# A ninth Strassen step in four projection units, and joins by transfer in the output units

## The chip, the cores and the metric

The kernel runs on one NeuronCore of a Trainium2 chip. TensorE (PE) multiplies: a stationary operand of 128x128 is loaded into its array (the trace shows these loads as PEld) and up to 512 columns stream past it into a bank of PSUM. VectorE (DVE) and ScalarE (ACT) work elementwise on SBUF and PSUM. SyncE (SP) issues the loads of the weights, GpSimd (POOL) issues most other transfers and runs a few small operations. Every engine takes its own instructions in order; they wait for each other by semaphores.

The metric is the device time of the program in microseconds (us), as the median of several runs.

## The reference

A decoder block for 256 tokens of width 4096, all in float32:

```python
h = rmsnorm(x, norm_w)
proj = h @ w_in                                    # 256 x 4096 times 4096 x 20480
u_p, z_p, u_c, b_c, c_c, z_c, g_logit = split(proj)    # six of 2048, one of 8192
y_pool = causal_multiscale_pool(u_p, pool_w, pool_scale) * silu(z_p)
y_conv = causal_gated_shortconv(u_c, b_c, c_c, conv_w, conv_b) * silu(z_c)
br = [y_pool @ w_branch[0], y_conv @ w_branch[1]]  # 256 x 2048 times 2048 x 4096, twice
merged = sum(sigmoid(g_logit + gate_b) * br)
out = rmsnorm(x + merged @ w_out, final_norm_w)    # 256 x 4096 times 4096 x 4096
```

The pooling averages over 2, 4, 8 or 16 trailing tokens by channel group, subtracts the token itself and applies a 512x512 matrix to each group. The short convolution has three taps.

## The kernel before

**Units and steps.** Every product is cut into units of 1024 output columns. Twenty units belong to `w_in` (`cz`, `cb`, `cu`, `cc` for the convolution, twice; `pz`, `pu` for the pooling, twice; `g0_0` to `g1_3` for the gates), eight to `w_branch` (`b0_0` to `b1_3`) and four to `w_out` (`o0` to `o3`). They run in that order. A unit of `w_in` or `w_out` has 16 steps, one for each pair of 128-row blocks of the inner dimension; a step loads one weight tile of 128 x 2048 (1 MB), which holds four quarters of 512 columns.

**Precision.** Each operand is split into a rounded high part and a low part, and each product takes three matmuls (high by high, high by low, low by high). For a weight tile ACT writes the high parts (`highs`, line 222, through `act`, line 60) and DVE the low parts (`lows`, line 226, through `sub`, which records at line 63).

**P and S steps.** A plain step (P) multiplies four quarters for two token halves: 8 groups of 3 matmuls. A Strassen step (S) forms four sums of the weight quarters and needs 7 groups of 3: M2, N3, M1, N7, N5, N6, N4, in this order unless it is the unit's last step. S uses the four operand entries of the pair of blocks themselves and four sums of them (Q3, Q5, Q6, Q7). For eight of the sixteen pairs of `x` (or of the merged tensor) the sums lie ready in `arena`; for the pairs 6 and 7 they can be put into a small tile `side`. The texts at the top name the order of steps: `EIGHT` has eight S of sixteen, `NINE`, `NINE_A` and `NINE_B` nine, `TEN` ten, `OUT3` seven, always with three P at its end.

**The ring.** High and low parts of weight quarters and of their sums go into a ring of `CELLS = 15` cells. A P step takes 4 cells, an S step 3 and then 4. Cells are given out in circular order and a request waits until all its cells are free (`Ring`, line 196). A cell is freed by the group that reads it last. `pump` (line 983) lays out the preparation of later steps as far ahead as cells allow, in program order, between the groups of matmuls. A P step right behind an S step is rounded in two halves.

**Joins.** The S products that belong to several quarters gather in four banks (`shared`); at a unit's end ACT copies them to a join slot, DVE forms three sums there (`corner_sums`), and `combine` (line 420) adds the slot to the unit's result. A unit marked `late` does this by two accumulating transfers from POOL, the others by an operation on DVE. A unit that `rotates` takes one of the three weight buffers (`raw`) as its slot; others use a tile of their own. `o0`, `o1` and `o2` rotate and are not late.

**Epilogues.** What follows a unit's end is a queue of small items, one taken at every sixth matmul (a tick), so that it runs beside the next unit. `gap(n)` are n empty ticks. In `g0_0`'s epilogue, which runs beside `g1_0`, the side sums of pair 6 and then of pair 7 are formed: a load of the pair into `sa` at once, scaling by ACT 8 ticks later, sums by DVE, and a store. In `pz0` and `pz1` the epilogue, beside `pu0` and `pu1`, builds the pooling bands; its last item are six small operations of DVE (line 75 and 629 in the trace).

**pu.** `pu0` and `pu1` have the text `EIGHT`. Side sums stand in `side` from `cz0` on, but the tile's place is given to the bands before `pu0`; the pooling itself (steps B and M) is multiplied inside `pz1` and `g0_0`.

**Fills.** The operands of the branch units and of the output units are refilled from memory through staging buffers (`sa`, and from `g1_3` on also `sb`): a transfer, four sums on DVE where the pair is an S pair, a rounding on ACT and a subtraction on DVE (`Fill`, line 768; `pop_fill`, line 799). `stages` (line 794) lists the buffers.

Of the kernel before, what the change touches and what calls it, by code (L numbers as in the profile page):

```python
# [44 lines left out]
TEN = "PSPSSPSSPSSPSSPS"  # L45
OUT3 = "PSPSPSPSPSPSSPPP"
B0 = "PPPPSPSP"
# [5 lines left out]
def hybrid_block(ctx: ExitStack, tc: tile.TileContext, x, xc, prm, rows_in, w_in, pool_w, w_branch, w_out, out):  # L53
# [185 lines left out]
    class Step:  # L239
        def __init__(self, unit, kind, src=None, op=None, **kw):  # L240
            self.unit, self.kind, self.src, self.op = unit, kind, src, op
            self.__dict__.update(kw)
            self.raw = None
            self.prepared = self.halved = False
            self.pre, self.mid = [], []

# [71 lines left out]
        def groups(self):  # L318
# [20 lines left out]
            else:  # L339
# [10 lines left out]
                for nm in order:  # L350
                    o, cell, bank = prods[nm]
                    ah, al = self.op.entry(o)
                    mm = [(ah, high(cell)), (ah, low(cell)), (al, high(cell))]
                    gs.append([bank, mm, [cell]])
            return gs

# [144 lines left out]

    def seq_x(text):
        if text is FIRST:
            return [("P", i) for i in FIRST]
        ns = text.count("S")
        if ns > NS + NB:
            ps, ss = list(range(16 - ns)), list(range(ND, 16)) + [ND - 1]
            if text is TEN:
                tens.append(text)
                ss = [ND - 2 + len(tens) % 2] + ss[:-1] + [ND - 1 - len(tens) % 2]  # L510
            return [(c, (ss if c == "S" else ps).pop(0)) for c in text]
        return sequence(text, ND, ND + NS + NB, NB)
# [3 lines left out]

    def in_unit(name, col, epi, text, **kw):
        units.append(Unit(name, lambda i: w_in[col // NU, i], seq_x(text), x_ops, epi, scaled=True, **kw))
        units[-1].text = text
        return units[-1]  # L520

    def side_items(i=ND - 1):
        def scaled():
            for k in range(2):
                v = sa[:, 6 - 2 * k:8 - 2 * k]
                act(v, v, scale=norm_col(2 * i + k))

        return [lambda: move(sa[:, 4:].rearrange("p o c -> p (o c)"), xc[i])] + gap(7) + [scaled, None, lambda: sums_s(sa)] + gap(3) + [
            lambda: act(side["tile"][:, 0], sa[:, 0:4]), None,
            lambda: sub(side["tile"][:, 1], sa[:, 0:4], side["tile"][:, 0].bitcast(F32))]  # L530

# [9 lines left out]
    def conv_units(c, first):  # L541
# [7 lines left out]
        def c_epi(u):  # L549
# [22 lines left out]
        u = in_unit(f"cz{c}", base + 3 * HALF, lambda u: silu_y(u.late) + (gap(4) + side_items() if first else []),  # L572
                    FIRST if first else SIX4, dst=Y)
# [106 lines left out]
    def gate_unit(n, c):  # L680
        def epi(u):
# [52 lines left out]
    def out_unit(c):  # L734
# [17 lines left out]

# [40 lines left out]

    stages = [sa]
    fills = deque()
# [3 lines left out]
    def pop_fill(force=None):  # L799
# [7 lines left out]
        if nxt is None or not nxt.ready() or now[0] < hush[0]:  # L807
            return
        st = next((q for q in stages if not any(q is u for u in used)), None)
        if st is not None:  # L810
# [115 lines left out]
    def before(i, fn, *args):  # L926
        steps[i].pre.append(item(fn, *args))

    for j in range(16):
# [163 lines left out]
    for u in units:  # L1093
# [3 lines left out]
        if not u.rotates:  # L1097
            u.join.slot = quarters(Y if u.name[0] == "g" else spare() if u.name[0] == "b" else E)
        if u is names["g1_0"]:
            bands_open.close()  # L1100
            open_side()
        if u is last_x:
            side["stack"].close()
            more = ctx.enter_context(tc.tile_pool(name="more", bufs=1))
            stages.append(more.tile([P, 8, P], F32, name="sb"))
            queue_fills()
        if u is last:
            break
        for st in u.steps:
            assert st.prepared, (u.name, st.kind)  # L1110
            run_step(u, st)
            if u.text is TEN and st.kind == "S" and st.op in x_ops[:ND] and st is not u.steps[-1]:
                move(side["tile"], side_d[ND - 1 - x_ops.index(st.op)])
            state["now"] += 1
# [114 lines left out]
```

## Time and profile before

| | |
|---|---|
| median of 3 runs | 2378.08 us (2377.83 to 2378.94) |
| the profiled run's own time | 2378.31 us |
| its span in the profile | 2376.6 us |
| granted TensorE clock, mean | 0.998 |
| PE busy | 2358.6 us (99%), 10466 matmuls |
| DVE busy | 2178.6 us (92%) |
| ACT busy | 1519.3 us (64%) |
| POOL busy | 116.8 us (5%) |
| read from memory, written | 522.51 MB, 27.26 MB |

The page of the profile gives busy time, share and number of instructions by engine, then the span in 40 slices (a digit is the busy share in tenths, PEclk the clock that PE was granted), then the chain of work that ended last. A row of a timeline reads: start in us, duration, engine, line of the program, operation, output and inputs with their shape, how many of them, and in brackets the idle time before with what ended it. The names are those of the program's tiles: `ring`, `raw` (weight buffers), `parts` (the sums of quarters), `arena` (operands), `sums` and `shared` (banks of PSUM). A wait row names who waited for whom, the total, how often, and the longest. Ends of matmuls are modelled, so a row of n matmuls that follow each other is read by the distance between starts.

### The profile page before, as it was taken

The page shows a single profiled execution, that of the slowest core. Times are in us where ns is not written, and L with a number is a line of the kernel's source. Part 1 is how long each engine was busy: PE and PEld are TensorE (multiplying, and loading weights), DVE is VectorE, ACT ScalarE, POOL GpSimd, SP SyncE. Part 2 cuts the span into 40 slices and gives each one's busy share as a digit, 9 for nine tenths or more (in the row PEclk, how much of TensorE's full clock was granted, in tenths as well). Part 3 has the DMA queues.
Part 4 walks back from the last instruction along what each step waited for, and adds up shares of the span by engine and source line. Part 5 has one row for each costly group of instructions (what it writes and reads, how often), then busy time and mean ns, then how long its engine had stood idle before and what let it go on. Part 6 is the DMA issues. An engine that isn't in the chain of part 4 may idle for free.

```text
span 2376.6 us, 28235 instructions
## 1 busy us (share of the span) xinstructions
PE 2358.6 (99%) x10466; PEld 1945.8 (82%) x10466; DVE 2178.6 (92%) x2378; ACT 1519.3 (64%) x1801; POOL 116.8 (5%) x181
## 2 busy tenths in 40 slices
PE   9999999999999999999999999999999999999998
PEld 7888888888888888888788888888888888888886
DVE  8889989989989969969899999998898799899998
ACT  6666656756656656656676767667665566566664
POOL 0000000000001000000000000001100000000000
PEclk9999999999999999999999999999999999999999
DMA  9656646756657546746877787778766666767767
GB/s 344 230 193 235 223 164 260 238 191 236 224 178 269 211 174 221 240 174 217 259 248 251 264 260 250 248 272 274 267 253 242 248 237 239 257 211 252 259 218 267
DMA packets 91322, 564.20 MB, mean 237 GB/s; under 512 B 10096, under 2 KB 10352, under 8 KB 30256
## 3 DMA queue, kind: packets, MB, share of 16 engines
q1 hardware_dynamic: 69824, 485.39, 56.5%
q0 software_dynamic: 20784, 75.77, 11.9%
q8 instruction: 82, 1.34, 0.2%
q10 hardware_dynamic: 576, 1.24, 0.1%
q14 instruction: 56, 0.46, 0.1%
HBM read 522.51 MB, written 27.26 MB: 231 GB/s over the span
## 4 chain that ended last, share of the span: by engine, by line
PE 94%; DVE 3%; DMA 1%; ACT 1%; issue 0%; POOL 0%; SPq 0%; DVEq 0%; ACTq 0%; POOLq 0%
PE sums L1021 69%; PE shared L1021 23%; DVE ring L63 1%; PE shared L665 1%; PE shared L458 1%; DMA sa<-in_xc_dram 1%; DVE parts L63 1%; DMA raw<-in_w_in_dram 1%; ACT ring L60 0%; DVE E L63 0%; DVE raw L63 0%; ACT E L60 0%; DVE E L75 0%; ACT raw L60 0%; PE shared L641 0%
## 5 line engine op out<-in xcount | busy, mean ns | idle before, releaser
L1021 PE MATMUL sums<-ring,arena 128*128 128x512 f32 x7215 | 1687.1, 390 | 4.2 <-DVE ring L63 1.8
L1021 PEld LDWEIGHTS sums<-ring,arena 128*128 128x128 f32 x7215 | 1352.8, 188 | 288.4 <-DVE ring L63 3.1
L63 DVE TENSOR_TENSOR ring<-raw,ring 128x1024 fp32r<-128x1024 f32 (+3 forms) x879 | 971.9, 1126 | 137.2 <-ACT ring L60 136.1
L60 ACT ACTIVATE ring<-raw 128x1024 fp32r<-128x1024 f32 (+3 forms) x682 | 796.2, 1202 | 251.7 <-PE sums L1021 101.2
L60 ACT ACTIVATE ring<-parts 128x512 fp32r<-128x512 f32 (+1 forms) x638 | 476.5, 761 | 475.1 <-DVE parts L63 413.8
L1021 PE MATMUL shared<-ring,arena 128*128 128x512 f32 x2169 | 523.2, 389 | 0.3 <-DVE ring L63 0.3
L63 DVE TENSOR_TENSOR ring<-parts,ring 128x1024 fp32r<-128x1024 f32 (+1 forms) x442 | 492.0, 1158 | 6.1 <-ACT ring L60 6.1
L1021 PEld LDWEIGHTS shared<-ring,arena 128*128 128x128 f32 x2169 | 407.0, 188 | 85.5 <-DVE ring L63 0.8
L63 DVE TENSOR_TENSOR parts<-parts,raw 128x512 f32<-128x512 f32 x416 | 286.6, 689 | 0.0
L63 DVE TENSOR_TENSOR parts<-raw 128x1024 f32<-128x1024 f32 x208 | 254.0, 1221 | 5.5 <-DMA raw<-in_w_in_dram 5.4
L1021 PE MATMUL sums<-ring,last_pair 128*128 128x512 f32 x336 | 84.6, 396 | 0.8 <-DVE ring L63 0.8
L1021 PEld LDWEIGHTS sums<-ring,last_pair 128*128 128x128 f32 x336 | 63.1, 188 | 16.3 <-DVE ring L63 1.2
L1021 PE MATMUL shared<-ring,last_pair 128*128 128x512 f32 x192 | 47.6, 397 | 0.0
L1021 PEld LDWEIGHTS shared<-ring,last_pair 128*128 128x128 f32 x192 | 36.1, 188 | 8.7
L60 ACT ACTIVATE E<-sums 128x512 f32<-128x512 f32 x72 | 39.7, 595 | 5.5 <-PE sums L1021 3.6
L60 ACT ACTIVATE E<-sums,rin 128x512 f32<-128x512 f32 x28 | 17.7, 689 | 29.3 <-PE sums L1021 29.3
L1021 PE MATMUL shared<-ring,side 128*128 128x512 f32 x135 | 34.0, 396 | 0.0
L63 DVE TENSOR_TENSOR raw<-raw 128x512 f32<-128x512 f32 (+1 forms) x27 | 23.5, 870 | 9.8 <-ACT raw L60 8.9
L1021 PEld LDWEIGHTS shared<-ring,side 128*128 128x128 f32 x135 | 25.4, 188 | 6.0
L60 ACT ACTIVATE last_pair<-shared 128x512 f32<-128x512 f32 x44 | 23.9, 596 | 9.4 <-PE shared L458 8.9
L63 DVE TENSOR_TENSOR E<-E,Y 128x2048 f32<-128x2048 f32 x13 | 29.8, 2290 | 0.1
L63 DVE TENSOR_TENSOR E<-E,last_pair 128x2048 f32<-128x2048 f32 x12 | 27.4, 2286 | 2.2 <-ACT E L60 2.2
(134 smaller groups left out, 717.1 us busy)
## 6 DMA issues: line engine op xcount, KB each, us to landing
raw<-in_w_in_dram SPq DMA_DIRECT2D x318, 1024.0 KB, 4.9
raw<-in_w_branch_dram SPq DMA_DIRECT2D x64, 1024.0 KB, 4.9
raw<-in_w_out_dram SPq DMA_DIRECT2D x64, 1024.0 KB, 5.1
E<-in_rows_dram POOLq DMA_DIRECT2D x16, 512.0 KB, 9.8
gates_d<-E POOLq DMA_DIRECT2D x8, 1024.0 KB, 6.1
E<-Y POOLq DMA_DIRECT2D x14, 512.0 KB, 8.2
Y<-E POOLq DMA_DIRECT2D x10, 512.0 KB, 8.1
y_d<-E POOLq DMA_DIRECT2D x8, 512.0 KB, 6.4
```

The lines of the kernel that those rows point to most:

```text
L60: return pin(nc.scalar.activation(dst, src, func, **kw))
L63: return pin(nc.vector.tensor_tensor(out=dst, in0=a, in1=b, op=op))
L458: pin(nc.tensor.transpose(shared(j)[:, i * T + t * P:i * T + (t + 1) * P], src[:, t, c:c + P], ident))
L665: pin(nc.tensor.matmul(o, a, b, start=(k, i) == (0, 0), stop=(k, i) == (3, 2)))
L1021: pin(nc.tensor.matmul(ps, lhs, rhs, start=n == 0, stop=n == u.total[b] - 1))
```

## The change

Five things are changed.

1. `pu0` and `pu1` get the text `NINE_B`. The ninth S step uses pair 7; `at=4` puts it in fifth place among the S steps, which is the ninth step of the unit and stands behind another S step. Its four sums are loaded by POOL from `side_d[1]` into one ring cell (`stream`); the cell is allotted before the step ahead of it and freed with the step's last group. `cz0`'s epilogue now also stores the sums of pair 7 to `side_d[1]`.
2. In `g0_0`'s epilogue only pair 6 is worked; its load stands `HUSH` = 14 ticks later, and pair 7 is loaded ready-made at the end.
3. `o1` and `o2` get `NINE`, with pair 7's sums in a `side` tile that is filled during `o1`; `OUT3` gets an eighth S, so that three S steps follow each other.
4. `o0`, `o1` and `o2` no longer rotate and become late: the slot is `Y`, and two transfers add it to the result. The final weights' row is loaded into `Y` later, and the squares come 8 ticks later.
5. From `g1_3` on half of `Y` serves as a third staging buffer for 40 ticks.

```diff
-OUT3 = "PSPSPSPSPSPSSPPP"
+OUT3 = "PSPSPSPSSPSSSPPP"
...
                 for nm in order:
                     o, cell, bank = prods[nm]
-                    ah, al = self.op.entry(o)
+                    if self.streamed is not None and o < 4:
+                        c = slice(o * P, (o + 1) * P)
+                        ah, al = ring[:, self.streamed, 0, c], ring[:, self.streamed, 1, c]
+                    else:
+                        ah, al = self.op.entry(o)
                     mm = [(ah, high(cell)), (ah, low(cell)), (al, high(cell))]
                     gs.append([bank, mm, [cell]])
+                if self.streamed is not None:
+                    gs[-1][2].append(self.streamed)
...
+            if at:
+                ss.insert(at, ss.pop())
...
             lambda: act(side["tile"][:, 0], sa[:, 0:4]), None,
-            lambda: sub(side["tile"][:, 1], sa[:, 0:4], side["tile"][:, 0].bitcast(F32))]
+            lambda: sub(side["tile"][:, 1], sa[:, 0:4], side["tile"][:, 0].bitcast(F32)),
+            lambda: move(side_d[i - ND + 2], side["tile"])]
...
-        in_unit(f"pu{c}", c * NU, lambda u: [], EIGHT).urgent = lambda: None
+        in_unit(f"pu{c}", c * NU, lambda u: [], NINE_B, at=4).urgent = lambda: None
...
             if (n, c) == (0, 0):
-                sides = []
-                for i in range(ND - 2, ND):
-                    sides += side_items(i) + [lambda i=i: move(side_d[i - ND + 2], side["tile"])]
-                items += gap(len(sides) - len(items))
+                sides = gap(HUSH) + side_items(ND - 2) + [lambda: side_load(ND - 1)]
...
-            return gap(1) + [lambda: row(0), lambda: row(1)] + gap(14) + [
+            return gap(2) + [lambda: row(0), lambda: row(1)] + gap(12) + [start] + gap(8) + [
                 lambda: square(0), lambda: square(1),
                 lambda: mul(E, E, Y[:, 0:1].to_broadcast([P, 2, NU])), lambda: move(o_d[c], E)]
 
-        text = (SIX5, EIGHT, EIGHT, OUT3)[c]
-        units.append(Unit(f"o{c}", lambda i: w_out[c, i], seq_x(text), m_ops, epi, before=start))
+        text = (SIX5, NINE, NINE, OUT3)[c]
+        u = Unit(f"o{c}", lambda i: w_out[c, i], seq_x(text), m_ops, epi, before=start if c == 3 else None)
+        u.late, u.rotates = c < 3, c == 3
+        units.append(u)
...
+    def stream(step, src):
+        def fetch(cells):
+            step.streamed = cells[0]
+            move(ring[:, cells[0]], src.rearrange("p a o c -> p a (o c)"))
+        steps[steps.index(step) - 1].pre.append((1, None, fetch))
+
+    for c in range(2):
+        for st in names[f"pu{c}"].main:
+            if st.kind == "S" and st.op is x_ops[ND - 1]:
+                stream(st, side_d[1])
...
         if not u.rotates:
-            u.join.slot = quarters(Y if u.name[0] == "g" else spare() if u.name[0] == "b" else E)
+            u.join.slot = quarters(Y if u.name[0] in "go" else spare() if u.name[0] == "b" else E)
+        if u is names["o1"]:
+            assert not fills
+            more.close()
+            open_side()
+
+            j, items = ND - 1, list(queue)
+            queue.clear()
+            sides = (gap(HUSH) + [lambda: move(sa[:, 4:].rearrange("p o c -> p (o c)"),
+                                                   m_d[j // 4][:, j % 4].rearrange("p k t -> p (k t)"))] + gap(8) + [
+                lambda: sums_s(sa), None, None, lambda: act(side["tile"][:, 0], sa[:, 0:4]), None,
+                lambda: sub(side["tile"][:, 1], sa[:, 0:4], side["tile"][:, 0].bitcast(F32))])
...
-            stages.append(more.tile([P, 8, P], F32, name="sb"))
+            stages.append((more.enter_context(tc.tile_pool(name="more", bufs=1)).tile([P, 8, P], F32, name="sb"), None))
+            stages.append((Y[:, 0].rearrange("p (o c) -> p o c", c=P), now[0] + 40))
             queue_fills()
```

More of the change, by code (lines that the diff above doesn't have):

```diff
@@ L244, in __init__ @@
             self.prepared = self.halved = False
+            self.streamed = None
             self.pre, self.mid = [], []
@@ L500, in sequence, with seq_x @@
         return [(c, (ss if c == "S" else ps).pop(0)) for c in text]
-    def seq_x(text):
+    def seq_x(text, at=None):
         if text is FIRST:
@@ L515, in seq_y, with in_unit, side_load, side_items @@
         return sequence(text, 8 - text.count("S"), 8, 0)
-    def in_unit(name, col, epi, text, **kw):
-        units.append(Unit(name, lambda i: w_in[col // NU, i], seq_x(text), x_ops, epi, scaled=True, **kw))
+    def in_unit(name, col, epi, text, at=None, **kw):
+        units.append(Unit(name, lambda i: w_in[col // NU, i], seq_x(text, at), x_ops, epi, scaled=True, **kw))
         units[-1].text = text
         return units[-1]
-    def side_items(i=ND - 1):
+    def side_load(i):
+        move(side["tile"], side_d[i - ND + 2])
+    def side_items(i):
         def scaled():
@@ L570, in c_epi @@
             return items + [lambda: move(E, g_d[c])] + gap(6) + [lambda: mul(E, E, Y), lambda: put(y_d[1, c], chan(E))]
-        u = in_unit(f"cz{c}", base + 3 * HALF, lambda u: silu_y(u.late) + (gap(4) + side_items() if first else []),
+        u = in_unit(f"cz{c}", base + 3 * HALF, lambda u: silu_y(u.late) + (gap(4) + side_items(ND - 1) if first else []),
                     FIRST if first else SIX4, dst=Y)
@@ L792, in advance @@
             return True
-    stages = [sa]
+    stages = [(sa, None)]
     fills = deque()
@@ L808, in pop_fill @@
             return
-        st = next((q for q in stages if not any(q is u for u in used)), None)
+        st = next((q for q, t in stages if (t is None or now[0] < t) and not any(q is u for u in used)), None)
         if st is not None:
@@ L1097, in hybrid_block @@
         if not u.rotates:
-            u.join.slot = quarters(Y if u.name[0] == "g" else spare() if u.name[0] == "b" else E)
+            u.join.slot = quarters(Y if u.name[0] in "go" else spare() if u.name[0] == "b" else E)
[9 more added lines that the diff above has]
+                lambda: sub(side["tile"][:, 1], sa[:, 0:4], side["tile"][:, 0].bitcast(F32))])
+            items += gap(len(sides) - len(items))
+            sides += gap(len(items) - len(sides))
+            queue.extend([lambda a=a, b=b: (a and a(), b and b()) for a, b in zip(items, sides)])
         if u is names["g1_0"]:
@@ L1103, in hybrid_block @@
             side["stack"].close()
-            more = ctx.enter_context(tc.tile_pool(name="more", bufs=1))
-            stages.append(more.tile([P, 8, P], F32, name="sb"))
+            more = ExitStack()
+            ctx.enter_context(more)
+            stages.append((more.enter_context(tc.tile_pool(name="more", bufs=1)).tile([P, 8, P], F32, name="sb"), None))
+            stages.append((Y[:, 0].rearrange("p (o c) -> p o c", c=P), now[0] + 40))
             queue_fills()
@@ L1112, in hybrid_block @@
             if u.text is TEN and st.kind == "S" and st.op in x_ops[:ND] and st is not u.steps[-1]:
-                move(side["tile"], side_d[ND - 1 - x_ops.index(st.op)])
+                side_load(2 * ND - 3 - x_ops.index(st.op))
             state["now"] += 1
```

## The prediction

> **What bounds the kernel now.** I read the page's busy times and slices first, then the chain that ended last, then what the matmul engine waited for, and last the timeline around those waits.
>
> ```profile
> span 2376.6 us, 28235 instructions
> PE 2358.6 (99%) x10466; PEld 1945.8 (82%) x10466; DVE 2178.6 (92%) x2378; ACT 1519.3 (64%) x1801; POOL 116.8 (5%) x181
> PE   9999999999999999999999999999999999999998
> PEclk9999999999999999999999999999999999999999
> PE 94%; DVE 3%; DMA 1%; ACT 1%; issue 0%; POOL 0%; SPq 0%; DVEq 0%; ACTq 0%; POOLq 0%
> ```
> ```profile
> PE sums L1021 <- DVE ring L63: 2.6, 4, 0.8
> PE sums L1021 <- ACT E L60: 1.4, 1, 1.4
> PE shared L857 <- DVE warm L853: 1.1, 1, 1.1
> PE sums L1021 <- DVE ring L760: 1.1, 1, 1.1
> ```
>
> (Waiter, whom it waited for, us in all, times, the longest.) PE is busy in every slice, and these waits come to 6.2 us; what else it waits for is below half a microsecond each. Time can only come from fewer matmuls or from those waits, and it is lost wherever DVE or ACT hands a weight tile over late. The program around this span took 2378.31 us, 1.7 more than the span and 0.23 above the median of 2378.08.
>
> The unit prices come from a regular stretch of pu0: one PE pass, one S step on DVE from 815.35, and the P step behind it.
>
> ```profile
> 807.20 2.88 PE L1021 MATMUL shared<-ring,arena 128*128 128x512 f32 x12
> 809.92 7.64 PE L1021 MATMUL sums<-ring,arena 128*128 128x512 f32 x33
> 811.88 0.28 DVE L75 SCALAR_TENSOR_TENSOR edge<-ident,sa 128x128 fp32r<-128x128 f32 x1
> 813.08 2.35 DVE L63 TENSOR_TENSOR ring<-raw,ring 128x1024 fp32r<-128x1024 f32 x2
> 813.57 1.06 ACT L60 ACTIVATE ring<-raw 128x1024 fp32r<-128x1024 f32 x1 [1.26 <-issue]
> 815.35 1.21 DVE L63 TENSOR_TENSOR parts<-raw 128x1024 f32<-128x1024 f32 x1
> 817.69 1.21 DVE L63 TENSOR_TENSOR ring<-raw,ring 128x1024 fp32r<-128x1024 f32 x1
> 819.43 2.35 DVE L63 TENSOR_TENSOR ring<-parts,ring 128x1024 fp32r<-128x1024 f32 x2
> 821.70 2.35 DVE L63 TENSOR_TENSOR ring<-raw,ring 128x1024 fp32r<-128x1024 f32 x2
> 823.97 1.21 DVE L63 TENSOR_TENSOR parts<-raw 128x1024 f32<-128x1024 f32 x1
> ```
>
> A matmul starts every (809.92-807.20)/12 = 0.2267 us. A P step (24) takes PE 5.44, an S step (21) 4.76. DVE takes 821.70-815.35 = 6.35 for an S step and 823.97-821.70 = 2.27 for a P step. Within an S step the low parts of the loaded quarters are done 817.69+1.14-815.35 = 3.48 after its start (1.14 is half of 821.70-819.43), those of the first two sums 5.22 after it. So P+S leaves DVE 1.6 us of room in 10.2, S+S+P (15.0 against 14.96) none.
>
> **Part 1, fewer matmuls.** Five steps become S: one each in pu0, pu1, o1, o2, o3. 5 x 3 x 0.2267 = -3.40 us. That is 0.14%; a kernel of this length can be told from no change from about 0.2% (4.8 us) on.
>
> **Part 2, the x pair's load.** In g1_0 this stands now:
>
> ```profile
> 1126.59 2.44 POOL L87 DMA_DIRECT2D E<-Y  x2 [53.47 <-DVE Y L63]
> 1128.08 1.53 POOL L84 DMA_DIRECT2D sa<-in_xc_dram  x1
> 1143.08 0.91 ACT L60 ACTIVATE sa<-sa,par 128x256 f32<-128x256 f32 x2 [8.08 <-DMA sa<-in_xc_dram]
> 1145.40 0.69 DVE L63 TENSOR_TENSOR ring<-raw,ring 128x512 fp32r<-128x512 f32 x1 [7.35 <-ACT ring L60]
> 1147.89 1.43 PE L1021 MATMUL sums<-ring,arena 128*128 128x512 f32 x5 [0.56 <-DVE ring L63]
> 1150.56 2.12 PE L1021 MATMUL shared<-ring,arena 128*128 128x512 f32 x8 [0.34 <-DVE ring L63]
> 1164.40 1.43 PE L1021 MATMUL sums<-ring,arena 128*128 128x512 f32 x5 [0.60 <-DVE ring L63]
> 1190.68 1.43 PE L1021 MATMUL sums<-ring,last_pair 128*128 128x512 f32 x5 [0.79 <-DVE ring L63]
> ```
>
> The load goes out behind two accumulating transfers and lands only at 1143; ACT, in order, waits 8.08 us, DVE behind it 7.35, and PE pays 0.56+0.34+0.60+0.79 = 2.29 us. POOL has nothing to hold it between the join and the load, so the load goes out as early as before; but ACT's scaling stands 14 ticks (14 x 6 x 0.2267 = 19 us) later and finds it landed. The second pair's sums are no longer formed there. DVE gets 7.35 us back against 2.29 lost: -2.29, bounds 0 and -2.29. On POOL the side store, the side load and the gates' store now follow each other; the side tile is wanted only in the unit's last step, some 75 us in.
>
> **Part 3, the streamed cell in pu.** The ninth S step is the unit's ninth step and follows an S step. Its side sums take one ring cell, allotted ahead of the step before: 1 + 7 + 7 = 15, the whole ring. The next cell in the ring, which the P step behind needs first, is the streamed cell itself. That P step is laid only behind the S step's last group, and in the changed order ACT's first rounding of it waits for the second matmul of group N6, the last group but one. Today a P step is ready 7 us ahead: the low parts that end at 823.97 are for the P step that PE reaches at 809.92 + 0.68 + 2 x (5.44+4.76) = 831.0. Worked from the end of N6's second matmul, call it 0 (PE still has 1+3 matmuls, until 0.91):
> - ACT's 128x1024 rounding (1.06) ends at about 1.3, with 0.16 for the matmul's drain (12 matmuls show 2.88 us against 12 x 0.2267 = 2.72) and an estimated 0.1 for the signal; PE's first matmul of the P step starts there, 0.4 late.
> - DVE's low parts (1.21) end at 2.55; PE's second matmul waits for them instead of starting at 1.13. Lost: 1.45 us.
> - DVE then does the rest of the P step (to 3.6), S (to 9.95), S: low parts of the loaded quarters at 13.43, PE there at 12.8. Lost: 0.69.
> - Both DVE steps end at 16.3; then the band building (813.08-811.88 = 1.20 us, the last entry of the queue, which stands behind these two steps), then the next P step's first low parts at 18.7; PE there at 18.2. Lost: 0.51.
> - From there P and S alternate and DVE gains.
>
> 2.65 us a unit, +5.30 for two. Bounds: the first wait alone (2.90) and, if the release is seen only at the step's last matmul, 0.91 more each (7.1). I take 5.30, since the order fixes the first wait and DVE's rows the other two. POOL: the streamed transfer waits for its cell with the band building's selects behind it; these have
>
> ```profile
> POOL sa L620 <- DVE cnt L613: 69.0, 2, 35.8
> side<-side_d POOLq DMA_DIRECT2D x5, 512.0 KB, 13.7
> E<-Y POOLq DMA_DIRECT2D x14, 512.0 KB, 8.2
> E<-in_x_dram POOLq DMA_DIRECT2D x6, 512.0 KB, 11.2
> ```
>
> 34 us to spare. The cell comes free after two groups of the fifth step and is first read in the second group of the ninth: (18+21+24+21+3) x 0.2267 = 19.7 us, against 13.7 for the like transfer. Hidden, with 6 us of cover.
>
> **Part 4, joined out units.** DVE loses the 2.28 us add at each join and the raw slot comes free; POOL gets two transfers from Y to E, then the x rows: 8.2 + 11.2 us. Issued about 5 us into the unit they land at 24.6; the squares stand at tick 25 (34 us). Hidden, by 9 us. What DVE has to carry:
>
> ```profile
> 1206.70:1287.30 80.60, 80.60 (x355) 66.45 (x354) 80.53 (x90) 56.80 (x70) 5.31 (x6) 1.00 0.79 258
> 2119.30:2201.10 81.80, 81.80 (x362) 67.62 (x361) 77.05 (x82) 52.01 (x65) 2.88 (x4) 1.00 0.70 240
> 2126.61 2.28 DVE L63 TENSOR_TENSOR E<-E,raw 128x2048 f32<-128x2048 f32 x1
> 2342.50 2.37 DVE L63 TENSOR_TENSOR ring<-raw,ring 128x1024 fp32r<-128x1024 f32 x2
> 2348.12 6.28 PE L1021 MATMUL sums<-ring,arena 128*128 128x512 f32 x27
> ```
>
> (Windows: length, then PE, weight loads, DVE, ACT.) o1 has 77.05 us of DVE in 81.8; less 2.28, plus 6.35-2.27 for the ninth S, plus 1.7 for the side sums: 80.5 in 81.1. The first row, a TEN unit with the same kind of join, has 80.53 in 80.60 and no PE wait: 0. In o3 three S steps follow each other. One more S puts DVE 4.08 + 0.68 = 4.8 us later against PE at the tail, if nothing of its lead is idle; the first tail step's low parts are ready 3.9 us ahead now (2344.9 against 2348.12 + 0.68). 0, since some of that lead is waiting for cells; bounds 0 and +0.9.
>
> The Trainium skill, page "SBUF — State Buffer", section "SBUF: two separate sides", says the opposite of a POOL transfer beside a busy DVE: while DVE holds the port pair it shares with GpSimd, the descriptors of such transfers cannot be written, and the transfer waits. The 8.2 us above is already measured beside a DVE as busy as that, so the trace does not bear out more; by the page's example (0.62 us becoming 3.1) the 19.4 us would be an estimated 97 and no unit would hold it. That is rival C.
>
> **Part 5, a third staging buffer.** Fills for the branch operands run earlier in g1_3, so b0_0 holds one more Strassen fill. Its end is the one place where PE waits for ACT:
>
> ```profile
> 1725.53 1.01 DVE L63 TENSOR_TENSOR sb<-sb 128x128 f32<-128x128 f32 x4
> 1733.81 0.69 DVE L63 TENSOR_TENSOR arena<-sa,arena 128x512 fp32r<-128x512 f32 x1
> 1735.18 7.14 PE L1021 MATMUL sums<-ring,arena 128*128 128x512 f32 x30 [1.35 <-ACT E L60]
> ```
>
> In the new order the 0.6 us subtraction of 1733.81 moves ahead of the next S step's sums, which hold up ACT's evacuation: +0.6. Bounds -1.35 (the wait goes) and +1.7 (0.6 plus that fill's 1.0).
>
> **Sum.** -3.40 - 2.29 + 5.30 + 0 + 0.6 = +0.2: 2378.31 becomes 2378.5 in a profiled run, 2378.3 against the median.
>
> **Rivals.**
> - A, the ring does not choke. For it: TEN units run S S P at a full DVE with no wait. Against: the 15 cells and the order. Then -3.40-2.29+0.6 = -5.1: 2373.0.
> - B, the streamed transfer is late, slower. It decides from 19.7 us on; 14.9 us were taken by the x pair's load behind two transfers (1128.08 to 1143). At twice 13.7, PE waits 7.7 us in each pu: +15, 2393. By the Trainium skill, "TensorE: Matmul & The Clock Gate", Part 1, PE idle beyond a window of some 3.4 us also halves the clock; the 1.35 us wait here left it at 9 in every slice, so no run here shows it.
> - C, the joins are late, slower. The squares stand in ACT's order ahead of ring roundings; if the two transfers take over 28.8 us instead of 19.4, ACT waits as at 1143, where 8.08 us of ACT cost PE 2.29. Three units: +6.9, 2385.2. Against: the gate units, whose joins go the same way.
> - D, g1_0 still waits (for example on the rescaling and side sums that fall together): +2.29, 2380.6.
>
> **Chances.** Forecast with its bounds, D within it: 0.68. A with a vanished wait in b0_0: 0.09. B 0.06, C 0.09, several small waits in o1 to o3 that pass 4.8 us: 0.08. The forecast's own range: 2378.1-5.7+2.9-1.35 = 2374.0 to 2378.1-3.4+7.1+1.7 = 2383.5; with the edge of C 2384.5, and of A 2373.5. Faster by over 0.2%: A, 0.09. Slower: B, C and the small waits, 0.23. Within: 0.68.
>
> **What would show it.** In pu0 and pu1: a P step after the ninth step with two PE waits for ACT ring and DVE ring, about 0.4 and 1.0, then one of 0.7 and one of 0.5; DVE idle about 7 us ahead of them. In g1_0: no ACT wait for sa and no PE wait. In o1 to o3: no PE wait. At b0_0's end: 1 to 3 us for ACT E. I am wrong if pu shows no wait, if PE waits for a transfer, or if the gate unit's waits stay.

## The result and the profile after

The changed kernel takes 2383.27 us (median of 20 runs, from 2381.81 to 2385.51) against 2378.89 us before: a ratio of 1.0019, 95% interval 1.0012 to 1.0026, so 4.4 us slower, at the edge of what can be told from no change. The forecast was 2378.3 us, 0.2 us slower than before. Its range of 2373.5 to 2384.5 holds the time, the forecast itself is 5.0 us too low; 0.8 of these are the kernel before, whose median was 2378.08 in the three runs that the prediction started from.

The page of the changed kernel, the lines that answer to those quoted of before (span; busy times; slices of PE's clock; chain that ended last):

```profile
span 2383.5 us, 28277 instructions
PE 2357.8 (99%) x10451; PEld 1943.6 (82%) x10451; DVE 2191.0 (92%) x2408; ACT 1531.1 (64%) x1813; POOL 122.7 (5%) x190
PEclk9999999999999999999999999999999999999999
PE 23%; DVE 3%; DMA 1%; issue 0%; ACT 0%; DVEq 0%; ACTq 0%; SPq 0%
```

The chain adds up to 27% of the span only: it breaks off at a link that the profile doesn't show, and nothing below rests on it. Fifteen matmuls are gone, as they should, but PE is busy for only 0.8 us less instead of 3.4, and the span is 6.9 us longer. (The time around this execution was 2385.41, among the slowest of the kernel; the sum at the end of the account below comes back to it.) What PE waited for:

```profile
PE sums L1044 <- ACT E L60: 4.7, 2, 4.4
PE sums L1044 <- DVE ring L63: 4.5, 6, 1.8
```

One wait of 4.4 us for ACT stands out; before it was 1.4. The others in the regular stretches are 0.76 us at most; longer ones, up to 1.8, stand only in the first 20 us, which vary from one execution to the next.

To place the 6.9 us I took the start of the same matmul in both traces and compared the lengths of the stretches between them. They agree within 0.02 us in all stretches that the change doesn't touch.

| stretch | matmuls gone | us more or less |
|---|---|---|
| start | 0 | +0.4 |
| pu0, pu1 | 6 | +2.23, +2.63 |
| g1_0 | 0 | -3.47 |
| end of b0_0 | 0 | +5.77 |
| b1_3 and o0 | 0 | +0.39, -0.10 |
| o1, o2 | 6 | -0.57, -0.58 |
| o3, to its last matmul | 3 | -0.70 |
| from the last matmul of the tail to the end | 0 | +0.86 |

(The expectations below name such stretches by units. They were counted in matmuls, and from `pu0` on their bounds lie off the units' own: the one called b1_0 holds the end of b0_0, those called g1_0 and g0_1 share g1_0, and the -0.68, -0.60 and +0.87 of o1, o3 and the tail are those of the table where they are cut at the units' own bounds.)

**The end of b0_0**, in the timeline of the changed kernel (start, duration, engine, line, operation; in brackets the idle time before it and what ended it):

```profile
1727.10 2.35 DVE L63 TENSOR_TENSOR ring<-raw,ring 128x1024 fp32r<-128x1024 f32 x2
1728.83 1.90 ACT L60 ACTIVATE ring<-raw 128x2048 fp32r<-128x2048 f32 x1
1729.32 6.28 PE L1044 MATMUL sums<-ring,arena 128*128 128x512 f32 x27
1730.75 2.29 DVE L63 TENSOR_TENSOR ring<-raw,ring 128x2048 fp32r<-128x2048 f32 x1 [1.30 <-ACT ring L60]
1732.96 1.08 DVE L63 TENSOR_TENSOR arena<-sb,arena 128x896 fp32r<-128x896 f32 x1
1733.97 0.68 DVE L63 TENSOR_TENSOR arena<-sa,arena 128x512 fp32r<-128x512 f32 x1
1734.57 1.22 DVE L63 TENSOR_TENSOR parts<-raw 128x1024 f32<-128x1024 f32 x1
1738.84 0.63 ACT L60 ACTIVATE ring<-parts 128x512 fp32r<-128x512 f32 x1 [1.13 <-DVE parts L63]
1739.38 2.04 ACT L60 ACTIVATE E<-sums 128x512 f32<-128x512 f32 x4
1740.01 9.85 PE L1044 MATMUL sums<-ring,arena 128*128 128x512 f32 x30 [4.41 <-ACT E L60]
```

The same places in the kernel before:

```profile
1723.25 2.36 DVE L63 TENSOR_TENSOR ring<-raw,ring 128x1024 fp32r<-128x1024 f32 x2 [0.39 <-ACT ring L60]
1729.73 1.22 DVE L63 TENSOR_TENSOR parts<-raw 128x1024 f32<-128x1024 f32 x1
1734.55 2.04 ACT L60 ACTIVATE E<-sums 128x512 f32<-128x512 f32 x4
```

The evacuation that PE waits for (`E<-sums`: ACT copies the unit's sums out of the banks that PE writes next) stands in ACT's order behind a rounding of the next S step, and that behind DVE's sums for it. These begin at 1734.57; before, at 1729.73, with PE 1.77 us earlier, so they are 3.1 us later against PE, and so is all behind them (4.41 - 1.35). The rows say where the 3.1 us come from. DVE starts the low parts of 1727.10 2.1 us later against PE than those of 1723.25; 0.9 of it are four sums of a fill, which stood behind them before (1725.53 in the prediction's rows) and stand ahead of them now (1726.17). Then DVE idles 1.30 us, where it did these sums before: 0.4 more. Last, the subtraction of 1733.97 (0.6) is new ahead of 1734.57.

And the 30 matmuls after the wait take 9.85 us; before they took 7.14. The stretches of the same trace (length, PE, PEld, DVE, ACT, POOL, granted clock, DMA share, GB/s) show why:

```profile
1738.00:1740.00 2.00, 0.00 (x0) 0.00 (x0) 1.97 (x4) 1.16 (x3) 0.00 (x0) 0.76 0.07 10
1740.00:1742.00 2.00, 1.99 (x5) 1.61 (x6) 1.97 (x3) 2.00 (x4) 0.00 (x0) 0.50 0.83 344
1742.00:1744.00 2.00, 2.00 (x6) 1.53 (x5) 2.00 (x3) 1.31 (x2) 0.00 (x0) 0.50 0.41 172
1744.00:1746.00 2.00, 2.00 (x6) 1.57 (x5) 2.00 (x3) 0.00 (x0) 0.00 (x0) 0.53 0.00 0
1746.00:1748.00 2.00, 2.00 (x10) 1.62 (x9) 2.00 (x2) 0.80 (x1) 0.00 (x0) 1.00 0.61 102
```

The clock is granted at 0.50 until 1745.9, and the 30 matmuls take 2.7 us more for it. Slices of 60 us hide it: PEclk reads 9 throughout on the page.

**In pu0**, the P step after the ninth step:

```profile
804.84 0.84 PE L1044 MATMUL sums<-ring,arena 128*128 128x512 f32 x3
805.98 0.50 PE L1044 MATMUL sums<-ring,arena 128*128 128x512 f32 x1 [0.29 <-ACT ring L60]
807.24 6.87 PE L1044 MATMUL sums<-ring,arena 128*128 128x512 f32 x29 [0.76 <-DVE ring L63]
816.66 1.07 PE L1044 MATMUL sums<-ring,arena 128*128 128x512 f32 x4
818.26 1.43 PE L1044 MATMUL sums<-ring,arena 128*128 128x512 f32 x5 [0.53 <-DVE ring L63]
822.25 1.07 PE L1044 MATMUL sums<-ring,arena 128*128 128x512 f32 x4
823.47 6.88 PE L1044 MATMUL sums<-ring,arena 128*128 128x512 f32 x29 [0.16 <-DVE ring L63]
```

By starts, against 0.2267 us a matmul: 805.98 is 0.46 late, 807.24 another 1.03, 818.26 0.69, 823.47 0.31. That is the forecast chain (0.4, 1.0, 0.69, 0.51), with a shorter last link here. DVE stands idle for 6.07 us ahead of it, ACT for 7.12. In the listed idle times each wait looks smaller than it is.

**The tail.** DVE's last sums of the output:

```profile
2370.40 0.75 DVE L1211 TENSOR_SCALAR parts<-parts,rout 128x1024 f32<-128x1024 f32 x1
2371.07 0.68 DVE L63 TENSOR_TENSOR E<-sums,E 128x512 f32<-128x512 f32 x1
2372.39 0.68 DVE L63 TENSOR_TENSOR E<-sums,E 128x512 f32<-128x512 f32 x1
```

The two sums follow each other behind the scaling of the first half of the tokens; PE starts its last matmul at 2371.06, and the second sum comes 1.3 us after that. In the kernel before:

```profile
2363.46 0.69 DVE L63 TENSOR_TENSOR E<-sums,E 128x512 f32<-128x512 f32 x1
2365.51 0.69 DVE L63 TENSOR_TENSOR E<-sums,E 128x512 f32<-128x512 f32 x1 [0.64 <-PE sums L1021]
```

There the first of the two was over while PE still worked, and DVE waited for PE with the second.

### The profile page after: what moved, and what is told of

It is laid out like the page before. It is cut to its first block, busy times and chain, and to the rows that moved or that the text cites. A ratio compares the mean times of both kernels' runs of the same rounds, so it can differ in the third digit from the quotient of the medians.

```text
span 2383.5 us, 28277 instructions
## 1 busy us (share of the span) xinstructions
PE 2357.8 (99%) x10451; PEld 1943.6 (82%) x10451; DVE 2191.0 (92%) x2408; ACT 1531.1 (64%) x1813; POOL 122.7 (5%) x190
## 5 line engine op out<-in xcount | busy, mean ns | idle before, releaser
L60 ACT ACTIVATE ring<-parts 128x512 fp32r<-128x512 f32 (+1 forms) x651 | 488.7, 763 | 476.7 <-DVE parts L63 413.3
L63 DVE TENSOR_TENSOR ring<-parts,ring 128x1024 fp32r<-128x1024 f32 (+1 forms) x457 | 503.3, 1144 | 6.4 <-ACT ring L60 6.4
L63 DVE TENSOR_TENSOR parts<-raw 128x1024 f32<-128x1024 f32 x213 | 259.1, 1216 | 9.5 <-DMA raw<-in_w_in_dram 5.2
L87 POOL DMA_DIRECT2D E<-Y x20 | 24.5, 1430 | 364.5 <-DVE Y L63 364.5
L1044 PEld LDWEIGHTS shared<-ring,side 128*128 128x128 f32 x153 | 28.8, 188 | 6.8
L60 ACT ACTIVATE Y<-shared 128x512 f32<-128x512 f32 x56 | 30.4, 602 | 5.0 <-PE shared L465 4.2
L63 DVE TENSOR_TENSOR Y<-Y 128x512 f32<-128x512 f32 (+1 forms) x33 | 28.7, 869 | 1.7 <-ACT Y L60 0.2
```

Source lines behind the costliest of these rows:

```text
L60: return pin(nc.scalar.activation(dst, src, func, **kw))
L63: return pin(nc.vector.tensor_tensor(out=dst, in0=a, in1=b, op=op))
L87: return pin(nc.gpsimd.dma_start(dst, src, accum_op=ALU.add))
L1044: pin(nc.tensor.matmul(ps, lhs, rhs, start=n == 0, stop=n == u.total[b] - 1))
```

## The experiments

Each is compared with runs of the kernel before on the same chip: 2378.57 us for e1 to e4, 2378.66 for e5 to e8, 2378.39 for e9 to e11.

**e1: without the third staging buffer.**

```diff
-            stages.append((Y[:, 0].rearrange("p (o c) -> p o c", c=P), now[0] + 40))
```

> The changed kernel without its third staging buffer. My theory: the third buffer puts two more fills ahead of the last Strassen step of b0_0, and PE's wait there grew from 1.35 to 4.41 us with the clock row at 0.50 behind it; without the buffer the wait is 1.35 again and the clock row 1.00 throughout. b1_0 took 48.93 us against 43.17, so -5.8: 2383.3 becomes 2377.5. By the prediction's own price for this part (+0.6) it would be -0.6: 2382.7. Rival: the fills come late for another reason (the x pair's load or the shift in pu), the wait stays and the time is 2383.3.

2378.74 us, 1.0001 of before (0.9992 to 1.0010); the stretch is 43.24 us, and the clock is 1.00 until the end.

```profile
1736.66 7.14 PE L1044 MATMUL sums<-ring,arena 128*128 128x512 f32 x30 [1.42 <-ACT E L60]
```

The buffer makes the loss at b0_0's end: all 5.7 us of it in the trace. In the medians, each against its own runs of the kernel before, it is 4.2 (+4.4 becomes +0.2). The forecast's price for it (0.6) is refuted.

**e2: the third buffer alone, on the kernel before.**

```diff
+        st = next((q for q, t in stages if (t is None or now[0] < t) and ...
+            stages.append((Y[:, 0].rearrange("p (o c) -> p o c", c=P), now[0] + 40))
```

> The kernel before with the third staging buffer and nothing else. My theory: the buffer alone makes the wait at b0_0's end: +5.8, 2378.9 becomes 2384.7, with a PE wait for ACT E of about 4.4 us there and a stretch at a clock of 0.50. By the prediction's price: +0.6, 2379.5. Rival: it takes the rest of the change as well, no more than 1.35 us of wait: 2378.9.

2382.31 us, 1.0018 (1.0009 to 1.0027). Timeline, and stretches of 2 us with the clock in the third column from the end:

```profile
1737.23 8.71 PE L1021 MATMUL sums<-ring,arena 128*128 128x512 f32 x30 [3.44 <-ACT E L60]
```
```profile
1738.00:1740.00 2.00, 2.00 (x6) 1.60 (x5) 2.00 (x3) 2.00 (x4) 0.00 (x0) 0.50 0.98 414
1740.00:1742.00 2.00, 2.00 (x8) 1.54 (x7) 2.00 (x3) 0.53 (x1) 0.00 (x0) 0.75 0.04 16
```

The buffer alone is enough: +3.7 us, with a wait of 3.44 us and 3.4 us at half clock. The size was not as expected (5.8): the wait is 1 us shorter than in the changed kernel and the clock low for half as long. Over all traces with the buffer and without a pause the stall is 3.4 to 4.4 us, with the matmuls that e7 and e11 put into it counted in. It varies with the execution: e7 and e11 run the changed kernel's program up to that place, and theirs is 3.8.

**e3: the streamed step in pu between two P steps.**

```diff
-        in_unit(f"pu{c}", c * NU, lambda u: [], NINE_B, at=4).urgent = lambda: None
+        in_unit(f"pu{c}", c * NU, lambda u: [], NINE_B, at=7).urgent = lambda: None
```

> The changed kernel with the streamed S step of pu0 and pu1 as the unit's fourteenth step, between two P steps, in place of the ninth behind an S step; number of steps, matmuls and transfers are the same. My theory: the ring then has to hold 1 + 4 + 7 = 12 cells, not 15, and nothing waits. The two units took 2.91 and 3.31 us more than their matmuls' change: -6.2, 2383.3 becomes 2377.1, with no PE wait in pu. Rival: not the ring but DVE's load (nine S steps) makes the waits, which then only move: 2383.3. Rival: only the first wait of each unit goes (0.29 + 0.76 listed, of 1.74): about -3.7, 2379.6.

2380.37 us, 1.0009 (1.0000 to 1.0018): 3 us of the 6.2 come back, in the median and in the trace.

```profile
828.81 2.53 ACT L60 ACTIVATE ring<-raw 128x1024 fp32r<-128x1024 f32 x3 [6.12 <-issue]
829.90 1.23 DVE L63 TENSOR_TENSOR ring<-raw,ring 128x1024 fp32r<-128x1024 f32 x1 [5.51 <-ACT ring L60]
837.53 0.73 PE L1044 MATMUL sums<-ring,last_pair 128*128 128x512 f32 x2 [0.82 <-DVE ring L63]
```

My theory of 12 cells falls. The ring gives out cells in turn, so a P step's four cells behind 1 + 4 + 7 others come round to the streamed cell (1 + 4 + 7 + 4 = 16 of 15) and wait until the streamed step's last groups give it free: ACT and DVE stand still for 6.12 and 5.51 us, so it isn't DVE's load, the first rival. Only the P step's first half is in time, and the S step behind it pays (1.52 and 1.56 us a unit by starts).

**e4: the x pair's load alone, on the kernel before.**

```diff
...
-                sides = []
-                for i in range(ND - 2, ND):
-                    sides += side_items(i) + [lambda i=i: move(side_d[i - ND + 2], side["tile"])]
...
+                sides = gap(HUSH) + side_items(ND - 2) + [lambda: side_load(ND - 1)]
```

> The kernel before with only the x pair's load changed in g1_0 (scaling 14 ticks on, the second pair loaded formed). By the lengths of g1_0 and g0_1 in the two traces: 83.54 + 81.69 became 81.12 + 80.65, so -3.5: 2378.9 becomes 2375.4. By the idle times that the prediction added up: -2.3, 2376.6. Rival: the gain hangs on the rest of the change and is 0: 2378.9.

2376.25 us, 0.9989 (0.9981 to 0.9998). The waits in g1_0 are gone and the two stretches are 3.47 us shorter in the trace, as in the changed kernel; the median fell by 2.3 only. The profiled execution, whose time is the median itself, was 1.1 us later than the kernel before when its first 30 us were over, with a stretch at half clock in them (below), and 0.2 us later by all the rest; so its span is 2.15 us shorter and not 3.47. Whether the other executions lost their 1.2 us there too, no run tells. The only one of the eleven with a mean clock of 0.999 took 2374.80 us, 3.5 under the median of the kernel before at that clock (2378.34).

**e5: two buffers, the streamed step last in pu, and another order in o3.**

```diff
-OUT3 = "PSPSPSPSSPSSSPPP"
+OUT3 = "PSPSSPSSPSSPSPPP"
-        in_unit(f"pu{c}", c * NU, lambda u: [], NINE_B, at=4).urgent = lambda: None
+        in_unit(f"pu{c}", c * NU, lambda u: [], NINE_B).urgent = lambda: None
-            stages.append((Y[:, 0].rearrange("p (o c) -> p o c", c=P), now[0] + 40))
```

> The changed kernel without the third buffer, with the streamed S step as the last step of pu0 and pu1, and with o3 in the order PSPSSPSSPSSPSPPP (eight S steps as before, no three in a row, one P step between the last S step and the tail). My theory for pu, after e3: the ring hands cells out in turn, so the next P step's four cells take in the streamed one wherever it stands, and their second half waits until the streamed step's last group; what follows decides the cost: S steps in e1 (2.9 and 3.3 us), one P and one S step in e3 (1.5 each), here P and band steps of pz1 and g0_0, in which DVE has room: 0 to 0.3 a unit, so -6 against e1. For o3: the tail's loss of 0.9 us goes. 2378.7 becomes 2372.0. Rival: the closing step's evacuations stand ahead of the second half on ACT and PE waits 1.5 us in pz1 and in g0_0: 2375.0. Rival for o3: DVE is as late at the end in any order: 0.9 more in either case.

2374.70 us, 0.9983 (0.9974 to 0.9991). The tail's loss is gone (-0.02 against +0.86); in the six traces with three S steps in a row it is 0.4 to 0.9, in the four with this order under 0.1. In pu0 and pz1 the streamed cell costs 0.55 us, in pu1 and g0_0 1.59, most of it in one wait:

```profile
1033.36 5.51 PE L1044 MATMUL sums<-ring,arena 128*128 128x512 f32 x23 [0.96 <-DVE ring L63]
2043.71 2.29 DVE L63 TENSOR_TENSOR E<-E,last_pair 128x2048 f32<-128x2048 f32 x1 [2.04 <-DMA last_pair<-gates_d]
```

2.14 us paid for 1.36 of matmuls saved, where 0 to 0.6 were expected: nine steps in pu do not pay even here. The second row is a late transfer in o0 that cost this execution 1.2 us; of the other traces only e11's has it, at 0.6.

**e6: the out units alone.** The kernel of e1 with pu and the x pair as before:

```diff
...
+                sides = []
+                for i in range(ND - 2, ND):
+                    sides += side_items(i)
...
-                sides = gap(HUSH) + side_items(ND - 2) + [lambda: side_load(ND - 1)]
-        in_unit(f"pu{c}", c * NU, lambda u: [], NINE_B, at=4).urgent = lambda: None
+        in_unit(f"pu{c}", c * NU, lambda u: [], EIGHT).urgent = lambda: None
...
-                stream(st, side_d[1])
```

> The changed kernel with pu0, pu1 (eight S steps, nothing streamed), the x pair's load and the staging buffers as before: only the out units are changed. By the prediction's steps 9 matmuls go and nothing else: -2.0, 2378.6 becomes 2376.6. By the unit lengths of the changed kernel: -0.10, -0.68, -0.57 in o0 to o2, -0.60 and +0.87 in o3 and the tail, +0.37 in b1_3: -0.7, 2377.9. Rival: the joins by transfers come late somewhere and cost more: over 2379.

2377.06 us, 0.9994 (0.9985 to 1.0003). By stretches o1 -0.58, o2 -0.57, o3 -0.67, tail +0.57; the joins by transfers cost nothing. The +0.37 in b1_3 is not here: it is in all seven traces with a streamed step in pu and in none without, and what carries it there stays open.

**e7 and e11: eight and sixteen matmuls into the wait at b0_0's end.**

```diff
+        if u.name == "b1_0":
+            o = u.main[0].op
+            for _ in range(8):        # e11: 16
+                pin(nc.tensor.matmul(shared(3), o.view[:, 0, 0], o.view[:, 0, 0:4], start=True, stop=True))
```

> The changed kernel with eight more matmuls (arena by arena, 128x512, into an idle bank, result unused) on PE at the place where it waits 4.41 us at b0_0's end; nothing waits for them and they take 8 x 0.2267 = 1.8 us of that wait. The weight tiles come no earlier, so by the wait alone nothing changes. My theory: the 30 matmuls behind the wait took 9.85 us instead of 7.14 because the clock was granted at 0.50 after PE had stood still for 4.41 us; with 2.6 us of idle time left the clock stays at 1.00 and they take 7.1: -2.7, 2383.3 becomes 2380.6. Here the Trainium skill, page TensorE: Matmul & The Clock Gate, Part 1, gives a window of about 3.4 us; 2.6 is below it. Rival: the slow stretch is one of late weights, and does not go: 2383.3. Rival: 2.6 us are enough to halve the clock too: 2383.3 with the clock row at 0.50.

> The changed kernel with sixteen matmuls in the wait at b0_0's end where e7 had eight: 3.6 us of the 4.41 are filled, some 0.8 us stay idle. What e7 and the other traces show of the granted clock: it goes to 0.50 for whole windows of 3.41 us after a window in which PE stood idle for 1.80 us or more, and not after 1.66 or less. Then it stays at 1.00 here and the 30 matmuls behind the wait take 7.1 us: -2.7 against the changed kernel, 2380.6, and about -1.5 against e7 in the span. Rival: the slow stretch is set by something else (late weights) and stays: 2382 or more.

e7, its timeline and its stretches:

```profile
1734.37 1.98 PE L1149 MATMUL shared<-arena 128*128 128x512 f32 x8
1738.14 8.70 PE L1044 MATMUL sums<-ring,arena 128*128 128x512 f32 x30 [1.80 <-ACT E L60]
```
```profile
1738.00:1740.00 2.00, 1.86 (x5) 1.53 (x6) 1.97 (x3) 2.00 (x5) 0.00 (x0) 0.62 0.83 287
1740.00:1742.00 2.00, 2.00 (x6) 1.52 (x6) 2.00 (x3) 1.44 (x2) 0.00 (x0) 0.52 0.49 205
```

e11, the same two views:

```profile
1734.98 3.79 PE L1149 MATMUL shared<-arena 128*128 128x512 f32 x16
1738.74 7.12 PE L1044 MATMUL sums<-ring,arena 128*128 128x512 f32 x30
```
```profile
1738.00:1740.00 2.00, 2.00 (x9) 1.35 (x8) 1.93 (x4) 2.00 (x5) 0.00 (x0) 1.00 0.73 233
```

My expectation for e7 fell: 1.80 us of idle time still halved the clock. With the wait filled (e11) PE goes on at full clock and the 30 matmuls take 7.12 us, so the slow stretch is PE's own clock and not late weights. e11's stretch is 3.5 us shorter than the changed kernel's: 2.7 for the clock, and 0.8 because the stall was shorter in this execution. The medians do not show it: 2381.08 (1.0010) for e7, 2381.89 (1.0013) for e11, where 2380.6 was expected of both. Neither is apart from the other, and the two profiled spans are alike (2379.9 and 2380.0), since e11's lost 0.6 us more at the start, 0.6 by the late transfer in o0 and 0.4 in the tail. That half clock makes the slow stretch rests on the traces; what the filling is worth in the median is not shown.

**e8: as e5, and the fills pause before b0_0's end.**

```diff
+            if u.name == "b0_0" and st is u.steps[4]:
+                quiet[0] = now[0] + 15
```

> As e5, and the fills for the branch operands pause from b0_0's fifth step to its end, so that 2.8 us of DVE work (sums, 128x896 and 128x512 subtractions) and two roundings on ACT stand behind the evacuation of b0_0's banks. My theory: the wait at b0_0's end is DVE's and ACT's order ahead of that evacuation; the 1.4 us that e1 and the kernel before show there go: -1.7 against e5 by b1_0's length (43.24 against 41.5). Rival: the fills are missed in b1_0, where PE then waits for an operand of its own: 0 or slower than e5.

2383.69 us, 1.0022 (1.0013 to 1.0031). The wait at b0_0's end is gone, -1.48 us against the kernel before and -1.55 against e5 (-1.7 was expected), so the order of DVE's and ACT's work ahead of the evacuation is its cause. The rival is right on the sum: the fills are missed in b1_0, which loses 10.3 us, part of it at a clock of 0.50 from 1759.5 to 1766.4.

```profile
1760.17 1.22 PE L1044 MATMUL sums<-ring,arena 128*128 128x512 f32 x2 [3.36 <-ACT arena L60]
1763.27 2.07 PE L1044 MATMUL sums<-ring,arena 128*128 128x512 f32 x4 [1.88 <-DVE arena L63]
1777.46 22.78 PE L1044 MATMUL sums<-ring,arena 128*128 128x512 f32 x99 [2.25 <-DVE arena L63]
```

**e9: the parts that pay.** As e5, pu as before.

```diff
-        in_unit(f"pu{c}", c * NU, lambda u: [], NINE_B).urgent = lambda: None
+        in_unit(f"pu{c}", c * NU, lambda u: [], EIGHT).urgent = lambda: None
```

> As e5 but with pu0 and pu1 as before (eight S steps, nothing streamed): the x pair's load, the joined out units with nine S steps in o1 and o2, o3 with eight in the order of e5, two staging buffers. My theory: a streamed cell costs more than the three matmuls it saves even as the last step (e5: +0.78 us over pu0 to g0_0 against the kernel before, the saving in it). By the traces: -3.5 for g1_0, -1.9 for o0 to o3, nothing at the tail, +0.4 at b1_3's end: -5.0, 2378.6 becomes 2373.6 and a PE wait of about 1.4 us stays at b0_0's end. Rival: the parts share a wait and do not add up: 2375 or more.

2372.87 us, 0.9978 (0.9968 to 0.9987). The parts add up, g1_0 -3.47 and o1 to o3 -1.81; the +0.4 that I had put down for b1_3 is not there.

**e10: e9 with the third buffer and the pause.**

```diff
+            stages.append((Y[:, 0].rearrange("p (o c) -> p o c", c=P), now[0] + 40))
+            if u.name == "b0_0" and st is u.steps[4]:
+                quiet[0] = now[0] + 15
```

> As e9 with the third staging buffer back and the pause of e8 (no fill advances from b0_0's fifth step to its end). My theory: e8's loss of 10.3 us came of fills that had no lead; with the third buffer the fill that the pause holds back is one further on, so it is not missed in b1_0, and what stood ahead of the evacuation stands behind it: no PE wait at b0_0's end, none in b1_0, -1.5 against e9: 2372.1. Rival: the held fills run beside b1_0's S steps and make DVE late there: as e9 or slower. Rival: the buffer costs at b0_0's end whatever the pause: 2379.

2372.13 us, 0.9973 (0.9963 to 0.9983): the fastest, 6.3 us under the kernel before.

```profile
1730.26 7.11 PE L1039 MATMUL sums<-ring,arena 128*128 128x512 f32 x30 [0.36 <-ACT E L60]
```

The buffer that cost 4 us costs nothing when its fills stay out of b0_0's last steps, and the fill it runs ahead is what e8 lacked (e8 differs in pu as well, far from here). Against e9 it is 0.7 us, half of what I expected, since 0.36 us of the wait is left and another 0.3 appears in b1_0; that the time is the expected 2372.1 is luck, e9 being 0.7 lower than expected.

## Why the forecast was 5 us low

**Part 5 failed.** It priced the third buffer at +0.6, with bounds of -1.35 and +1.7; in the traces of e1 and e2 it costs 5.7 and 3.7. The step looked at one instruction, the subtraction of 0.6 us that moves ahead of the next S step's sums. It left out that the other fill's four sums (1.0 us) move ahead too, and its rounding on ACT, for which DVE idles 1.30 us before 1730.75, and that DVE enters the stretch with less lead, by about 1 us. (e2, with the buffer alone, has all but this last: its wait is 3.44 and not 4.41.) And its upper bound took a longer wait at PE to cost its length only. Rival B did name what half a clock would do there, but asked it of pu, where no wait is long enough; at b0_0's end, with 1.35 us idle already, it had to be in the bounds. That the time still lies in the range is luck: part 5 passed its upper bound by 4.1 us, and the room for it came from part 2, whose gain the range's upper end had at 0.

**Part 1** holds but for a tenth of a microsecond a step: o1 and o2, where PE waits for nothing, are 0.57 and 0.58 us shorter where 0.68 was forecast. Matmuls that take their stationary operand from `side` start 0.233 us apart in the trace, those from `arena` 0.227, and an S step with `side` has twelve of them: 0.08. What makes them slower stays open.

**Part 2** has the right mechanism and too small a size: -3.47 for -2.29. The terms were listed idle times. By starts each of the four waits costs about 0.27 more: 0.16 by which the row of the last matmul runs on into the wait, and 0.11 at the restart, where the second matmul starts 0.34 us after the first (818.26 and 818.60 in pu0) and not 0.23; 2.29 + 4 x 0.27 = 3.37. Rival D is out, no wait is left in g1_0.

**Part 3** was right in kind and order: 2.91 and 3.31 us where 2.65 was forecast, again with 0.11 a wait left out, and with a last wait of 0.31 in pu0 and 0.73 in pu1 instead of 0.51. Rival A (no choke) is out, and so is B: the streamed transfers landed 4.1 us after their issue, where 13.7 was taken, and PE waits for no transfer. What I hadn't seen is that the place of the streamed step isn't the cause (e3, e5).

**Part 4** was right on the joins, with no PE wait for them, and DVE in o1 about as full as forecast (80.5 us):

```profile
2127.10:2208.20 81.10, 81.10 (x358) 66.96 (x357) 79.79 (x92) 54.00 (x67) 5.88 (x7) 1.00 0.78 257
```

Rival C is out: DVE at 79.79 us of 81.10 holds up no join, so the port rule of the Trainium skill's page "SBUF — State Buffer", section "SBUF: two separate sides", does not decide here. But the transfers were priced too low. Of the two of a join in o1 to o3 the first lands after 5.9 us and the second after 14.0 to 14.7; the 8.2 us taken is the median between two such groups, a time that none of the 14 of before has. In o1 the last x row lands 25.2 us after the first issue (2132.77 to 2158.01), not 19.4, and rival C begins at 28.8. At the tail I took 0 and the upper bound, +0.9, came true by another way, which is luck: the tile is in time, and DVE's last sums are late. One P step between the last S step and the tail cures it (e5).

**The sum.** 5.2 too little for part 5, 0.9 for part 3, 0.8 for o3 and the tail, 0.5 for b1_3 to o2, 0.4 at the start, less 1.2 in part 2, make 6.6 of the 6.7 us by which the profiled span missed. The median is 2.1 us below that execution; one stretch of half clock less would be 1.6 of it, but no trace shows which of the other executions had less.

## What to carry to other kernels

A change that only hands a buffer over earlier still reorders two in-order engines: follow the last evacuation of a unit through both queues and ask what now stands ahead of it, before pricing the buffer at the one instruction that moves. Price a wait of the matmul engine by the starts of its matmuls, and where one may come near 1.7 us, add the clock to its upper bound. Look at the single transfers before taking a median of them. A ring that gives out cells in turn charges a long-lived cell to whoever comes round to it, wherever it is put.

## What the runs showed of the hardware

The granted clock fell to 0.50 in whole units of 3.41 us (6.83 in the changed kernel, e3 and e8, 3.41 in e2, e4 and e7). Laid on a grid of that length through each of the 13 traces, every fall follows a length in which PE stood idle for 1.80 us or more, and none follows a length at full clock with 1.71 or less: half of it is the edge, as far as PE's modelled ends go. At half clock less is enough to stay there: lengths that hold 0.97, 1.66 and 2.19 us of idle time (the changed kernel, e3, e8) were followed by another. The Trainium skill, page "TensorE: Matmul & The Clock Gate", Part 1, gives a free-running window of 3413 ns, which these traces confirm (the changes of clock lie on the grid, and its place differs by execution), and the throttled state after an idle window of about 3.4 us; here the window need be idle by half only.

So the same idle time may cost nothing or 1.6 us, by where the grid's lengths begin. e4 and e10 both wait 1.82 to 1.83 us some 18 us after the start; the 14 matmuls behind it take 5.09 us in one and 3.47 in the other:

```profile
19.46 5.09 PE L1022 MATMUL sums<-ring,arena 128*128 128x512 f32 x14 [1.82 <-DVE ring L63]
```
```profile
19.49 3.47 PE L1039 MATMUL sums<-ring,arena 128*128 128x512 f32 x14 [1.83 <-DVE ring L63]
```
